# A hybrid recurrent layer on one core: the side chains between the projection matmuls are placed anew

## The chip, the core and the metric

One core of a Trainium2 chip runs the kernel. The metric is the device time of one execution in microseconds (us), the median of several runs; lower is better.

## What is computed

One step of a one-layer decoder on 2048 prompt tokens, 16 learned meta tokens in front of them, and 8 sample sequences of 4 tokens, at width 1024. The input is normalised, goes through one projection to the columns of four branches of width 256, each branch runs its own recurrence, is gated, and an output projection with a second normalisation ends the layer. All states go out too.

```python
hp = _layernorm(jnp.concatenate([meta, x_prompt], axis=1), ln_in_g, ln_in_b)
u = jnp.einsum('btd,de->bte', x, lw['w_in'])
...
# A: SSD, B: S5 diagonal SSM, C: gated DeltaNet, D: HGRN2; mix = their gated outputs
...
out = jnp.einsum('btc,cd->btd', mix, lw['w_out'])
x_new = _layernorm(DN_ALPHA * x + out, lw['ln_g'], lw['ln_b'])
```

Branch C, in a chunk, decays the products of its normalised keys and queries and inverts a triangular matrix:

```python
dec = jnp.exp(jnp.where(incl[:, :, None], diff, -jnp.inf))
kk = jnp.einsum('bcihd,bcjhd->bcijh', k, k)
m = jnp.where(strict[:, :, None], kk * dec * beta[:, :, :, None, :], 0.0)
tinv = lax.linalg.triangular_solve(eye + m, ...)
aq = jnp.einsum('bcihd,bcjhd->bcijh', q, k) * dec
```

Branch D multiplies queries and keys under a decay for each channel, and carries the state from chunk to chunk:

```python
a = jnp.einsum('bihk,bjhk,bijhk->bijh', qi, ki, dec)
o = (jnp.einsum('bijh,bjhv->bihv', a, vi)
     + jnp.einsum('bihk,bhkv->bihv', qi * jnp.exp(gi), s))
s = s * jnp.exp(gl)[..., None] + jnp.einsum('bjhk,bjhv->bhkv', ki * jnp.exp(gl[:, None] - gi), vi)
```

## The kernel before, in words

The tokens are worked off in two halves. Chunk 0 (48 tokens: meta tokens and all samples) and chunks 1 to 8 are the first half, chunks 9 to 16 the second. For each half `phase1a` normalises and transposes the input; `phase1b` runs the projection tile by tile (`proj`, L583): 128 output channels by blocks of some 300 to 512 tokens, 24 matmuls to a block (`pj`), each weight split into a high and a low part (L579, L580). Behind a block stand its consumers: the convolution and its activation (`conv_tile`, L641), copies to memory, gates. After both halves `out_chunk` runs the output projection.

Between the projection matmuls stand dependent chains of small work. They are generators, called jobs. A job yields the time until its next step may come, in microseconds of a planner's clock which adds an estimated cost for each TensorE instruction (`_pe`, L113); `poll` starts each step whose time has come, between two groups of three projection matmuls. So the yields set the place of each step among the matmuls. TensorE's instructions are pinned in the order in which they are written. The other engines and the DMA queue of SyncE are ordered by a scheduler, and each works off its own queue in order. When the program needs a job to be done, `drain` moves the clock on and puts the job's steps one behind the other, with no projection between.

The jobs that matter here:

- `gates` (L482): the gates of A and C for a half; sums of the logarithms over a chunk by TensorE (`g_g`), their exponentials as rows (`g_rw`), which go to memory as `rows_d`.
- `l2n` (L662): the norms of keys or queries of two heads: sums of squares (`l2p`), a power (`l2r`, L695 and L697), a transposition, a row to memory and back, a product (L713).
- `c_pre` (L730): for a pair of heads and each chunk, the decay matrix (`cdec`) is loaded from `rows_d`, masked on GpSimd (L725), exponentiated on ScalarE, and multiplied with the products of keys and queries (`cma`, L753); the result is stored to `ma_d`. After the second pair, `base_inv` (L761) loads the diagonal blocks of the matrices, inverts them on VectorE with two instructions per row (L787, L789), copies the result (L791) and stores it to `tb_d`. In the first half it does so twice, for the chunks ("main") and then for chunk 0 ("head").
- `right_jobs` (L1896): one sequence, each part behind the former: `b_setup` (branch B's matrices; the input matrices `W1` in four blocks `bs_wt`, L1070 to L1077), `b_tail` (chunk 0 of B), `b_main` (L1121 to L1169) twice, chunk 0 of D, D's groups of two chunks 1, 3, 5, 7, `b_main` twice, and in the second half D's groups 9 and 13 beside 11 and 15.
- `d_group` (L1576): D for a group. It loads queries with forget gates (`d_qf`), keys (`d_k`) and values, forms `d_pr` on GpSimd, the diagonal (`hsel`), and then goes through levels that double the block size: a product of `Q` and `d_k` on TensorE, a masked copy to `d_AT` (L1670), updates of `Q` and of the keys (L1666, L1667). Then for each chunk the keys are transposed and copied (`d_kt`), and outputs and the state `SD` follow. For chunk 0 `tail_state` (L1553) updates the nine segments' states in six parts: VectorE masks the values into a stage that takes `d_qf`'s buffer (L1564), one matmul (`d_qf`, `d_kt`), and an addition (L1573).

The last projection tile group of a half begins with a hook, `last`: it drains the inverse, in the first half also D's chunk 0, in the second half all of `right_jobs`.

Of the kernel before, what the change touches and what calls it, by code (L numbers as in the profile page):

```python
# [22 lines left out]
F32 = mybir.dt.float32  # L23
# [35 lines left out]
def tw(t):  # L59
    return 128 if t else HEAD  # L60
# [10 lines left out]
class Pinned:  # L71
    """An engine whose instructions don't move ahead of earlier ones."""
# [8 lines left out]
class Chain:  # L81
    """An engine whose instructions issued through here stay in the order in which they are written."""
# [14 lines left out]
class Kern:  # L97
# [12 lines left out]
    # The tensor engine runs in the order in which the kernel is written out. Dependent chains  # L110
    # are generators ("jobs") that yield the time until their next step can start; they are
    # woven between the matrix products of the projections.
# [64 lines left out]
    # ---------------------------------------------------------------- constants  # L177
    def consts(self, cp):
# [15 lines left out]
        # sums the two parts of 32 channels of a head  # L194
# [24 lines left out]
    # ---------------------------------------------------------------- phase 1  # L219
    def small_loads(self, cp):  # L220
        """Job: small parameters, and the conv histories of the sample sequences channel-major."""
        a, V = self.a, self.Vp
        yield 8.2
        # channel-major small parameters, through one transpose
# [29 lines left out]
        # HGRN2 lower bound: softmax over the single layer, cumulative sum minus the first entry  # L254
# [70 lines left out]
    def phase1a(self, half, xp):  # L325
        """Layer norm and transposition of the input, and the products whose results are wanted token-major.
        The first yield comes before anything that needs the space of xh, xl or the weight ring."""
# [46 lines left out]
        def weights(i, parts):  # L374
            """u | i, dt, a, b: high and low parts."""
# [23 lines left out]
        else:  # L399
            # the first tile waits for as little as possible: one row comes by DMA, the other through the tensor engine  # L400
# [81 lines left out]
    def gates_in(self, half, sp):  # L482
# [3 lines left out]
        o = 1 - half          # chunk 0, the tail, is the first of half 0  # L486
# [14 lines left out]
        # softplus = max(x, 0) + log1p(e), log1p(e) = 2 atanh(e / (2 + e))  # L501
# [20 lines left out]
        # beta = sigmoid  # L522
# [7 lines left out]
        # inclusive cumulative sums inside each chunk, and the chunk totals  # L530
        yield 19.0
# [19 lines left out]
        if o:  # L551
            # decays of the tail segments, on every partition
# [177 lines left out]
    def c_pre(self, p):  # L730
# [8 lines left out]
        for t in range(*TR[half]):  # L739
# [14 lines left out]
            for j in range(2):  # L754
                self.st(self.ma_d[t][:n, j, 2 * p:2 * p + 2, :n], ma[:n, j, :, :n])
# [1394 lines left out]
```

## Time and profile before

| | us |
|---|---|
| runs | 1456.67, 1447.78, 1452.73 |
| median | 1452.73 |
| span of the profiled execution | 1448.2 |
| TensorE busy | 1294.9 (89%) |
| VectorE busy | 934.2 (65%) |
| GpSimd busy | 616.3 (43%) |
| ScalarE busy | 536.1 (37%) |
| mean granted clock of TensorE | 0.936 of full speed |

The page does not list a time of the profiled execution besides its span; the span lies inside the range of the three runs. Busy time is the time in which an engine had an instruction at work. PE is TensorE, DVE VectorE, ACT ScalarE, POOL GpSimd, SP the engine that issues most transfers.

### The profile page before, as it was taken

Reading aid. Unit: us, or ns where it says so; the run is one execution under the profiler, and the core shown is the slowest. Engines: PE = TensorE matmul, PEld = TensorE weight load, DVE = VectorE, ACT = ScalarE, POOL = GpSimd, SP = SyncE. Lnnn points to the kernel's source line nnn. Section 1 sums busy time; section 2 is a strip of 40 time slices with the busy share of each in tenths; the row PEclk is TensorE's granted clock in tenths of the full one; section 3 lists DMA queues with packets and bytes.
Section 4 is the critical chain, followed back from the end, with each engine's and each line's share of the span. In section 5 each row is a group of like instructions: output and inputs, shape, how many; then the busy total and the mean of one; then the engine's idle time right before and its main releaser. Section 6 shows DMA issues by size and latency. Waiting matters only on the chain. (4 is left out here: it accounts for less than half of the span.)

```text
span 1448.2 us, 23800 instructions
## 1 busy us (share of the span) xinstructions
PE 1294.9 (89%) x8596; PEld 1090.3 (75%) x8596; DVE 934.2 (65%) x2173; ACT 536.1 (37%) x1010; POOL 616.3 (43%) x508
## 2 busy tenths in 40 slices
PE   7984898899898999998996888789997999999997
PEld 6974788878877999877674677677775677777776
DVE  8899524557978549474355789962345676665654
ACT  3224256545214342353543442242434332333211
POOL 4065322524433312152434443441324476676665
PEclk9997999999989999999998899899998899999999
DMA  8511552464337434215534633125649777676333
GB/s 211 192 49 36 127 143 57 140 189 114 106 97 203 145 104 153 77 39 158 157 87 121 201 102 95 44 88 145 177 124 251 196 198 190 198 182 184 111 105 113
DMA packets 259007, 195.79 MB, mean 135 GB/s; under 512 B 70950, under 2 KB 231928, under 8 KB 258873
## 3 DMA queue, kind: packets, MB, share of 16 engines
q1 hardware_dynamic: 258890, 194.28, 47.2%
q8 instruction: 68, 1.11, 0.3%
q14 instruction: 49, 0.39, 0.1%
HBM read 125.01 MB, written 64.31 MB: 131 GB/s over the span
## 5 line engine op out<-in xcount | busy, mean ns | idle before, releaser
L126 PE MATMUL pj<-xh,w 128*128 128x384 f32 (+2 forms) x1760 | 547.8, 379 | 10.8 <-ACT raw L635 5.5
L126 PEld LDWEIGHTS pj<-xh,w 128*128 128x128 f32 x1760 | 339.7, 200 | 57.4 <-issue 11.6
L126 PE MATMUL pj<-xl,w 128*128 128x384 f32 (+2 forms) x880 | 322.8, 367 | 0.0
L126 PEld LDWEIGHTS pj<-xl,w 128*128 128x128 f32 x880 | 176.3, 200 | 12.4 <-issue 0.5
L580 POOL TENSOR_TENSOR w<-wr,w 128x1024 fp32r<-128x1024 f32 x44 | 109.9, 2497 | 85.6 <-ACT w L579 68.0
L641 DVE SCALAR_TENSOR_TENSOR cv<-raw,par,cv 128x384 f32<-128x384 f32 (+2 forms) x150 | 130.5, 872 | 9.5 <-POOL cv L639 8.2
L126 PE MATMUL pj<-woh,o_mh 128*128 128x512 f32 (+2 forms) x280 | 116.6, 416 | 6.3 <-DVE xt L1846 3.2
L126 PE MATMUL pj<-wol,o_mh 128*128 128x512 f32 (+2 forms) x280 | 109.4, 391 | 6.2 <-POOL wol L1817 5.9
L126 PE MATMUL pj<-woh,o_ml 128*128 128x512 f32 (+2 forms) x280 | 109.4, 391 | 0.0
L126 PE MATMUL pj<-w,xh 128*128 128x256 f32 (+3 forms) x544 | 105.2, 295 | 0.0
L639 POOL TENSOR_SCALAR cv<-raw,par 128x384 f32<-128x384 f32 (+2 forms) x50 | 49.3, 986 | 119.0 <-ACT raw L635 95.4
L126 PEld LDWEIGHTS pj<-w,xh 128*128 128x128 f32 (+1 forms) x544 | 84.6, 189 | 1.2 <-ACT xh L88 0.8
L126 PE MATMUL pj<-w,xl 128*128 128x256 f32 (+3 forms) x272 | 78.0, 291 | 0.8 <-DVE xl L88 0.8
L725 POOL TENSOR_TENSOR cdec<-cdec,negm 128x256 f32<-128x256 f32 x32 | 29.4, 921 | 98.6 <-DMA cdec<-rows_d 63.1
L126 PEld LDWEIGHTS pj<-woh,o_mh 128*128 128x128 f32 (+1 forms) x280 | 52.3, 187 | 18.6 <-DVE xt L1846 4.0
L126 PEld LDWEIGHTS pj<-wol,o_mh 128*128 128x128 f32 (+1 forms) x280 | 52.5, 188 | 16.0 <-POOL wol L1817 6.9
L1789 DVE TENSOR_TENSOR y<-y,f_R 128x768 f32<-128x768 f32 (+1 forms) x17 | 27.1, 1591 | 56.0 <-POOL f_R L1788 50.9
L126 PEld LDWEIGHTS pj<-woh,o_ml 128*128 128x128 f32 (+1 forms) x280 | 52.2, 187 | 12.3 <-issue 0.7
L308 POOL TENSOR_TENSOR lnrs<-lnve,mhalf 128x1 f32<-128x1 f32 (+1 forms) x34 | 24.5, 720 | 74.0 <-DVE lnve L88 46.2
L813 ACT ACTIVATE zs<-pj 128x384 f32<-128x384 f32 (+2 forms) x40 | 20.8, 520 | 87.6 <-PE pj L126 72.8
L126 PEld LDWEIGHTS pj<-w,xl 128*128 128x128 f32 (+1 forms) x272 | 51.2, 190 | 1.5 <-DVE xl L88 1.3
L1788 POOL TENSOR_TENSOR f_R<-f_R,f_z 128x768 f32<-128x768 f32 (+1 forms) x17 | 30.2, 1778 | 51.1 <-DMA f_R<-r_d 32.5
(570 smaller groups left out, 2687.8 us busy)
## 6 DMA issues: line engine op xcount, KB each, us to landing
wr<-in_w_in_dram SPq DMA_DIRECT2D x46, 512.0 KB
xt<-in_x_prompt_dram SPq DMA_DIRECT2D x16, 512.0 KB
xn_d<-xt SPq DMA_DIRECT2D x16, 512.0 KB
ma<-cma SPq DMA_DIRECT2D x64, 128.0 KB
xt<-xn_d SPq DMA_DIRECT2D x16, 512.0 KB
out_dram<-xt SPq DMA_DIRECT2D x15, 512.0 KB
f_R<-r_d SPq DMA_DIRECT2D x32, 192.0 KB
cdec<-rows_d SPq DMA_DIRECT2D x32, 128.0 KB
```

The lines of the kernel that those rows point to most:

```text
L126: self._pe(self.PE.matmul(out, lhsT, rhs, start=start, stop=stop, **kw), 0.01 + n * (1 if rhs.dtype == F32R else 4) / 2400)
L308: self.G.tensor_tensor(rs[:n], ve[:n], self.mhalf[:n, 0:1], ALU.pow)
L580: self.G.tensor_tensor(w[:, :, 1], raw, w[:, :, 0].bitcast(F32), SUB)
L639: G.tensor_scalar(cv[:, 0:m], raw[:, 3:3 + m], w[3], b, op0=MUL, op1=ADD)
L641: V.scalar_tensor_tensor(cv[:, 0:m], raw[:, k:k + m], w[k], cv[:, 0:m], op0=MUL, op1=ADD)
L725: G.tensor_tensor(d[:n, :, :n], d[:n, :, :n], m[:n, None, :n].to_broadcast([n, nh, n]), ADD)
L813: S.activation(z, p, AF.Silu)
L1788: G.tensor_tensor(R[:, :, :n], R[:, :, :n], z[:, :, :n], MUL)
L1789: V.tensor_tensor(y6[:, 0:6, :n], y6[:, 0:6, :n], R[:, :, :n], MUL)
```

## The change

The decay of a chunk in `c_pre` is split in two: `decay_load` (the transfer) and `decay_end` (mask and exponential). The first chunk's is loaded and ended before the loop, and each further chunk's is loaded before the products of the former and ended behind them. In `d_group` the keys of all chunks of a group are transposed into one PSUM tile before the outputs; the first chunk's go into the buffer of `tots`. A group that follows another one waits 1.5 on the planner's clock before its first product, and not 8.0. Six yields of side chains are longer: the gates of the first half (19.0 to 25.0), `l2n` (3.7 to 6.0), the W1 blocks (2.6 to 6.5), `b_main` (17.1 to 19.5), D's step behind its first level (3.0 to 4.5), and `out_setup` for the first half of the output weights (8.9 to 16.0). Comments are taken out.

```diff
@@ gates
-        yield 19.0
+        yield 25.0 if o else 19.0
@@ l2n
-        yield 3.7
+        yield 6.0
         pt = self.pt()
         self.tr(pt[:2 * N, 0:128], rf)
@@ c_pre
-        yield 6.1
-        for t in range(*TR[half]):
+        a, b = TR[half]
+        raw = self.decay_load(self.fp, "cdec", a, 4 + 2 * p, 2)
+        yield 3.0
+        dec = self.decay_end(raw, a, 4 + 2 * p, 2)
+        yield 3.1
+        for t in range(a, b):
             n = tw(t)
             t0 = tof(t) - BASE[half]
-            dec = self.decay(self.fp, "cdec", t, 4 + 2 * p, 2)
-            yield 1.5
+            raw = self.decay_load(self.fp, "cdec", t + 1, 4 + 2 * p, 2) if t + 1 < b else None
...
+            if raw is not None:
+                yield 1.0
+                dec = self.decay_end(raw, t + 1, 4 + 2 * p, 2)
+                yield 1.5
@@ b_setup, the W1 blocks
             V.tensor_tensor(wt, wt, wu, ADD)
-            yield 2.6
+            yield 6.5
@@ b_main
-        yield 17.1
+        yield 19.5
@@ d_group
-        yield 13.6 if tail else 8.0
+        yield 13.6 if tail else 8.0 if first else 1.5
...
-            yield 3.0
+            yield 4.5 if s == 2 else 3.0
...
-        else:
+        kts = [tots[:, :, 0:128]] * (nch - 1) + [tp.tile([128, 2, 128], F32, name="d_kt" + sfx)]
+        p = self.pt()
+        for c in range(nch):
+            for g in range(2):
+                self.tr(p[:n, 256 * c + 128 * g:256 * c + 128 * g + 128], kS[:, g, n * c:n * c + n])
+            S.copy(kts[c][:n], p[:n, 256 * c:256 * c + 256].rearrange("p (g d) -> p g d", g=2))
+        yield 1.4
+        if not tail:
             yield from self.until(("d", t0c))
         for c in range(nch):
             t = t0c + c
             tk = slice(n * c, n * c + n)
-            p = self.pt()
-            for g in range(2):
-                self.tr(p[:n, 128 * g:128 * g + 128], kS[:, g, tk])
-            kt = tp.tile([128, 4, 64], F32, name="d_kt" + sfx)
-            S.copy(kt[:n].rearrange("p h d -> p (h d)"), p[:n, 0:256])
-            yield 1.4
+            kt = kts[c]
@@ out_setup
-            yield 8.9
+            yield 16.0 - 7.1 * half
@@ right_jobs
         def seq(ts, sfx):
-            for t in ts:
-                yield from self.d_group(t, 2, sfx)
+            for i, t in enumerate(ts):
+                yield from self.d_group(t, 2, sfx, i == 0)
```

On TensorE, early in the first half, the gates' sums (`g_g`), their rows (`g_rw`) and the W1 transposes (`bs_wt`) stand before as follows; `w_1229` and `w_1491` are the weights of two projection tiles that follow each other.

```order
L126 MATMUL pj<-xh,w_1229 128x384
L126 MATMUL pq<-g_g_1270,triu 128x64
L126 MATMUL pq<-g_g_1270,ones 128x64
...
L120 MATMUL pq<-ident,bs_wt 128x128 x4
...
L120 MATMUL pq<-ident,g_rw 128x128
L126 MATMUL pj<-xh,w_1229 128x384
...
L120 MATMUL pq<-ident,bs_wt 128x128 x4
```

Now, in the same stretch:

```order
L126 MATMUL pj<-xh,w_1491 128x304
L120 MATMUL pq<-ident,bs_wt 128x128 x4
L126 MATMUL pq<-g_g_1270,triu 128x64
L126 MATMUL pq<-g_g_1270,ones 128x64
...
L126 MATMUL pq<-l2p,sel_140 32x9 x8
...
L120 MATMUL pq<-ident,g_rw 128x128
...
L120 MATMUL pq<-ident,g_rw 16x128
L120 MATMUL pq<-ident,bs_wt 128x128 x4
```

All of them move behind matmuls of the next tile, the gates' sums 33 projection matmuls later, the four W1 blocks 27, 48, 69 and 93 later.

Late in the first half, on TensorE, D's chunk 0 (the transposes of its keys, its outputs with the state `S`, and the six products `d_qfa,d_kta` of `tail_state`) stands before like this; the five products that are left out here follow with 8 to 12 projection matmuls in front of each.

```order
L120 MATMUL pq<-ident,d_ka 48x128 x2
L126 MATMUL pj<-xh,w_4032 128x384
...
L126 MATMUL pq<-d_ATa,d_va 64x48 x4
L126 MATMUL pq<-d_pra,S_3929 128x16
...
L126 MATMUL pq<-d_qfa,d_kta 128x384
L126 MATMUL pj<-xh,w_4032 128x384
L126 MATMUL pj<-xl,w_4032 128x384
...
L126 MATMUL pq<-d_qfa,d_kta 128x384
```

Now:

```order
L126 MATMUL pq<-Qa,d_ka 16x16 x2
L120 MATMUL pq<-ident,d_ka 48x128 x2
L126 MATMUL pq<-d_ATa,d_va 64x48 x4
L126 MATMUL pq<-d_pra,S_4138 128x16
L126 MATMUL pq<-d_pra,S_4138 128x4 x8
L126 MATMUL pq<-d_pra,S_4138 128x16
L126 MATMUL pq<-d_pra,S_4138 128x4 x8
L126 MATMUL pq<-d_qfa,d_kta 128x384 x6
L126 MATMUL pj<-xh,w_4320 128x304
```

The last level, the transposes, the outputs and all six products stand together, at the place of the hook `last`, and no projection matmul is between them.

On VectorE at the same place, the end of the main inverse (128 partitions), the masks of `tail_state` (`d_qfa<-d_va,segmask`) and the head inverse (12 partitions) now come in this order:

```order
L803 TENSOR_TENSOR acc<-acc,cdec 128x31
...
L1587 TENSOR_TENSOR S_4138<-S_4138,pq 64x3x64 x2
L1578 TENSOR_TENSOR d_qfa<-d_va,segmask 48x384
L801 TENSOR_TENSOR cdec<-acc 12x15
L803 TENSOR_TENSOR acc<-acc,cdec 12x15
...
L801 TENSOR_TENSOR cdec<-acc 12x48
L1587 TENSOR_TENSOR S_4138<-S_4138,pq 64x3x64
L803 TENSOR_TENSOR acc<-acc,cdec 12x12x4
L1587 TENSOR_TENSOR S_4138<-S_4138,pq 64x3x64
L1578 TENSOR_TENSOR d_qfa<-d_va,segmask 48x384
```

Before, all six masks stood in front of the first operation of the head inverse; now four of them stand behind it.

## Rows read from the trace of the kernel before

**Rows 1.** Page, busy us, share of the span, instructions of an engine.

```profile
PE 1294.9 (89%) x8596; PEld 1090.3 (75%) x8596; DVE 934.2 (65%) x2173; ACT 536.1 (37%) x1010; POOL 616.3 (43%) x508
```

**Rows 2.** Waits of TensorE by what it waited for: us in total, times, longest.

```profile
PE pq L126 <- DVE Qa L1666: 16.7, 10, 6.4
PE pq L120 <- DVE bs_wt L1072: 13.3, 3, 8.3
PE pq L126 <- DVE b L1152: 12.2, 2, 9.2
PE pq L120 <- DVE l2r L697: 8.5, 3, 4.6
PE pq L126 <- DVE g_g L521: 7.4, 1, 7.4
...
PE pq L126 <- DVE cma L753: 5.7, 4, 2.4
...
PE pq L120 <- POOL l2r L695: 3.1, 1, 3.1
...
PE pq L126 <- DVE SD L1712: 3.0, 1, 3.0
```

**Rows 3.** Windows: length, busy us of each engine (instructions), granted clock, DMA share, GB/s.

```profile
100.00:125.00 25.00, 14.04 (x65) 12.51 (x63) 23.29 (x81) 9.59 (x20) 15.80 (x28) 0.80 0.08 21
125.00:150.00 25.00, 12.78 (x79) 11.58 (x79) 24.98 (x68) 11.34 (x22) 14.30 (x6) 0.80 0.14 37
...
350.00:375.00 25.00, 24.67 (x142) 22.04 (x140) 24.69 (x63) 9.83 (x21) 13.79 (x10) 1.00 0.48 143
375.00:400.00 25.00, 21.59 (x129) 20.23 (x129) 24.37 (x67) 6.89 (x21) 8.48 (x9) 0.83 0.24 76
...
1325.00:1440.00 115.00, 111.84 (x661) 90.56 (x659) 65.94 (x130) 23.92 (x30) 71.23 (x45) 1.00 0.39 118
```

**Rows 4.** Timeline of TensorE after the gates' sums: start, us, instruction.

```profile
120.84 0.84 PE L126 MATMUL pj<-xh,w 128*128 128x384 f32 x2
121.48 0.52 PE L126 MATMUL pj<-xl,w 128*128 128x384 f32 x1
...
122.39 0.52 PE L126 MATMUL pj<-xh,w 128*128 128x384 f32 x2
122.75 0.34 PE L126 MATMUL pj<-xl,w 128*128 128x384 f32 x1
```

**Rows 5.** Timeline of VectorE between 124 and 141 us.

```profile
124.00 5.43 DVE L641 SCALAR_TENSOR_TENSOR cv<-raw,par,cv 128x328 f32<-128x328 f32 x1
129.35 2.82 DVE L1072 TENSOR_TENSOR bs_wt<-bs_wt,bs_wu 128x512 f32<-128x512 f32 x1
...
140.65 0.67 DVE L1072 TENSOR_TENSOR bs_wt<-bs_wt,bs_wu 128x512 f32<-128x512 f32 x1
```

**Rows 6.** Timeline of GpSimd in the same stretch.

```profile
124.03 5.05 POOL L1061 TENSOR_TENSOR Pw<-Pw,bs_w 128x2304 f32<-128x2304 f32 x1
129.03 2.60 POOL L580 TENSOR_TENSOR w<-wr,w 128x1024 fp32r<-128x1024 f32 x1
```

**Rows 7.** Timeline of TensorE at D's chunk 0; in brackets the idle time before.

```profile
377.79 0.43 PE L126 MATMUL pq<-Qa,d_ka 128*48 128x48 f32 x4 [3.12 <-DVE Qa L1666]
...
413.25 0.88 PE L126 MATMUL pq<-d_qfa,d_kta 48*128 48x384 f32 x2 [1.95 <-DVE d_qfa L1564]
...
416.03 0.91 PE L126 MATMUL pq<-d_qfa,d_kta 48*128 48x384 f32 x2
...
418.64 0.91 PE L126 MATMUL pq<-d_qfa,d_kta 48*128 48x384 f32 x2
```

**Rows 8.** Timeline of VectorE: the main inverse's last operation, the head inverse's first.

```profile
407.50 0.19 DVE L789 TENSOR_TENSOR acc<-acc,cdec 128x31 f32<-128x31 f32 x1
...
419.19 0.16 DVE L787 TENSOR_TENSOR cdec<-acc 12x15 f32<-12x15 f32 x1
```

More of the change, by code (lines that the diff above doesn't have):

```diff
@@ L718, in decay, with decay_load @@
     def decay(self, pool, tag, t, rows0, nh, bufs=None):
-        S, G = self.S, self.G
+        return self.decay_end(self.decay_load(pool, tag, t, rows0, nh, bufs), t, rows0, nh)
+    def decay_load(self, pool, tag, t, rows0, nh, bufs=None):
         n = tw(t)
@@ L723, in decay, with decay_end @@
         self.ld(d[:n, :, :n], dap(self.rows_d, (t * 16 + rows0) * 128, [[0, n], [128, nh], [1, n]]))
+        return d
+    def decay_end(self, d, t, rows0, nh):
+        S, G = self.S, self.G
+        n = tw(t)
         m = self.negm if t else self.negm_t
@@ L1574, in tail_state, with d_group @@
                 yield 1.4
-    def d_group(self, t0c, nch, sfx):
+    def d_group(self, t0c, nch, sfx, first=True):
         V, S, G = self.V, self.S, self.G
@@ L1707, in d_group @@
                 for g in range(2):
-                    self.mm(su[:, g], kt[:n, 2 * g:2 * g + 2].rearrange("p h d -> p (h d)"), vf[:n, 128 * g:128 * g + 128])
+                    self.mm(su[:, g], kt[:n, g], vf[:n, 128 * g:128 * g + 128])
                 for g in range(2):
@@ L1731, in d_group @@
                 V.tensor_copy(cdd[:, :, 1:9], tot4[:, :, 4:12])
-                yield from self.tail_state(self.SD9, kt, vf,
+                yield from self.tail_state(self.SD9, kt.rearrange("p g (h d) -> p (g h) d", h=2), vf,
                                 lambda h, g: cdd[64 * h:64 * h + 64, g, :, None],
```

## Prediction, before the changed kernel ran

> **What bounds the kernel now.** I read the busy shares first, then the tensor engine's waits, then windows of 25 us, then single engines inside the windows that stand out. The shares say that TensorE is the bound: 89% of the span, against 65% for VectorE [rows 1]. Its instructions run in the order in which they are written, so a microsecond of its idleness is gained back only if the matmuls behind it move up. In the last stage it is busy 111.84 of 115 us at a granted clock of 1.00 [rows 3]; what is saved before comes out at the end. The waits name what the change aims at: Qa (the levels of branch D), bs_wt (the input matrices W1 of branch B), b (B's states), l2r (the norms), g_g (the gates), cma (the products of branch C) and SD (D's state) [rows 2]. The windows add a warning. Between 100 and 150 us TensorE is busy only 26.8 of 50, but VectorE 48.3, and between 350 and 400 VectorE is busy 49.1 of 50 [rows 3]. In such stretches TensorE waits because VectorE is late, and moving the waiting instruction back helps only as far as other matmuls don't depend on the same VectorE.
>
> **The change part by part.** All terms are in us on the profiled execution, whose page gives the span of 1448.2 alone; the three timed runs have a median of 1452.73, 4.5 above it.
>
> *Gates and W1, early.* Gone or moved: 7.4 (g_g) and 13.3 (bs_wt, three times), 20.7 together [rows 2]. The order shows the gates' sums behind 33 projection matmuls more, the W1 transposes behind 27 to 93 more. A pair of them lasts 0.84 us where one alone lasts 0.52, so they start 0.32 apart; two microseconds later it is 0.52 and 0.34, so 0.18 apart [rows 4]: half clock and full clock. At 0.18 the delays are 6 us for the gates and 5 to 17 for W1. But VectorE has the same 48 us to do. In its new order the copy that feeds g_rw stands some thirty rows of other work behind g_g, so I put a new wait of about 11 us on the g_rw transposes in its place. Net -10. Bounds: nothing gained, if VectorE sets this whole stretch, and 28 if all 20.7 go with the half-clock work after them. That work is visible in the same rows: six us after the wait on g_g the matmuls still start 0.32 us apart, which is some 3 us lost.
>
> Row first, for a rule on this place: the addition that ends a W1 block took 2.82 us at 129.35 and 0.67 at 140.65, and a convolution step 5.43 [rows 5]; the slow ones lie beside GpSimd's sum Pw (5.05) and its weight split (2.60) [rows 6]. The Trainium skill, SBUF — State Buffer, section "Who interferes with whom", says that a VectorE instruction with two SBUF inputs contends with a GpSimd instruction that reads SBUF, and that the second waits for the first to end. The trace agrees. By that rule a W1 addition may fall under Pw instead of under the weight split and this term would be about -8 instead of -10.
>
> *Norms.* l2r waits 8.5 in three places on VectorE and 3.1 once on GpSimd [rows 2]. The step is put 2.3 us later on the planner's clock, and in the second half the order leaves 27 matmuls instead of 9 or 15 between. Taking at most 2.3 to 3 from each: -8 (bounds 0 and -11.6).
>
> *States of B.* b waits 12.2 in two places, the longest 9.2 [rows 2]. Put 2.4 later: the short one (3.0) goes, the long one loses 2 to 3. -5 (bounds 0, -12).
>
> *Levels of D.* Qa waits 16.7 in ten places, the longest 6.4; one is the 3.12 at 377.79 [rows 2, 7]. The longer step after the first level lets twelve more matmuls in before the second, 2 us for each of three groups that wait there: -6 (bounds 0, -16.7).
>
> *Decay rows of C a chunk ahead.* The transfer, GpSimd's mask and the exponential leave the loop between two chunks. cma waits 5.7 in four places [rows 2], and part of it is the multiplication itself, which stays: -3 (bounds 0, -5.7).
>
> *Keys together, groups at once.* The same transposes and copies run, in one stretch rather than two; I put this itself at nothing, since neighbours cover them (bounds +2 and -2). D's chain ends earlier, so that the half's end need not drain it: SD's 3.0 [rows 2] go, -3. In return the next group's first product stands 21 to 30 matmuls behind the last of the former, and GpSimd must form d_pr in that time; where a weight split of 2.60 [rows 6] is in front, it is late. For three groups +2 (bounds 0, +8).
>
> *D's tail.* This is the price. B now delays D, and the diff's own delays add to it: the first product of chunk 0 moves five blocks of 24 matmuls back. Before, the six state updates stand with 8 to 12 matmuls between them. Now the last level, the transposes, the outputs and all six updates stand together in the drain that ends the first part, with no projection between. One update takes 2.61 from start to start (416.03 to 418.64), of which TensorE works 0.91 [rows 7], while VectorE adds the result and masks the next part: five gaps of 1.7 are 8.5 us idle. VectorE's order makes it worse: four of the six masks stand behind the first operation of the inverse for chunk 0, which waits until the main inverse has been copied, stored and read back. That took 11.5 us before (407.50 to 419.19) [rows 8]. About 6 us of other work stand in that gap now, so some 5 are added, and 3 for the last level and the transposes without cover: 16.5. What goes in return is 3.12 and 1.95 of idle time [rows 7] and less half-clock work, together 6.5. Net +10 (bounds 0 and +30, the latter if the main inverse is still running when TensorE arrives).
>
> *Output weights.* One step later on the planner's clock; the transfers that limit them are not moved. 0 (bounds -3, +3).
>
> Sum: -10 - 8 - 5 - 6 - 3 - 3 + 2 + 10 = -23, so 1425 for the span and, 4.5 above it, 1430 for the median.
>
> On the clock: the granted clock is 0.80 in the two windows with the long waits and 1.00 in the last stage [rows 3], that is, a part of them at 1.2 GHz and the rest at 2.4. The Trainium skill, TensorE: Matmul & The Clock Gate, section "HAM oscillation — how this bites in real kernels", says that an engine which waits falls back to the lower clock and pays for it in the work behind. By that rule a vanished wait gives more than its length, and the sum would be near -30; but the new drain would be charged the same way, and the trace shows both.
>
> **The rivals.**
> 1. *All named waits vanish.* Gates, W1, norms, b's short wait, D's levels and SD give 20.7 + 11.6 + 5 + 10 + 3, and TensorE, whose work is 1294.9 [rows 1], simply closes up; the drain costs 10. That is -40, a median of 1412. For it: VectorE has 35% of the span free. Against it: not where these waits are [rows 3].
> 2. *VectorE keeps its pace.* The matmuls are written earlier or later, but between 100 and 150 and between 350 and 400 VectorE finishes when it did. Early gains (-10, -8 in half) are then waited out at the next consumer, and what is left, some -12 of the later terms, pays the drain: 1450. For it: 48.3 and 49.1 busy of 50 [rows 3]; against it, VectorE has room over the whole span [rows 1], so that a stretch which ends late is made up behind it.
> 3. *The drain swallows it: slower.* TensorE comes to the drain earlier by the 15 to 20 us gained, while the main inverse, which VectorE works off in one piece with little spare, ends when it did, at 407.5 [rows 8]. TensorE then waits these 15 to 20 out as well, adds 16.5 of drain and some 5 of half-clock work, and only the later terms (about -12) stand against it: +15 to +20 once the upstream gain is gone, a median near 1468. It decides from where TensorE arrives more than some 15 us before the inverse's last operation. Against it: the inverse also waits for fewer competitors, since D's tail no longer lies inside it.
> That the change does not do what it says I leave out: the order shows each part.
>
> **How the numbers follow.** The forecast (-10 to -32) gets 0.50, rival 1 0.12, rival 2 0.24, rival 3 0.14. About 1% (14.5 us) is what a measurement of this kernel can tell from no change. Faster by more: four fifths of the forecast's case, all of rival 1 and a little of rival 2, 0.54. Slower by more: most of rival 3, 0.12. Within: 0.34. The likeliest case's own range is 1420 to 1444; the wide one runs from 1405 (rival 1 with some of the clock) to 1462 (the lower half of rival 3).
>
> **What would show it.** Right: g_g and bs_wt gone from the list of waits with one on g_rw of 5 to 15 in their place; l2r under 4; the wait on b under 8; Qa under 10; and a new group of waits on d_qfa and S inside one stretch of some 25 us, late in the first half, where projections stop. Wrong: no such stretch, or one of 40 us with the wait on the inverse's operations; a span of 100 to 150 that is as long as before (rival 2); waits on d_pr of more than 8 in all.

## The result, and the profile after

The changed kernel is slower: 1515.54 us (1514.12 to 1518.32), against 1454.7 for the kernel before (1447.78 to 1461.62), a ratio of 1.043 with an interval of 1.037 to 1.050. Its profiled execution has a span of 1513.9, 65.7 more than the 1448.2 of before. The forecast was 1430 with a range up to 1462.

The page's first part, to be read beside [rows 1]:

```profile
span 1513.9 us, 23785 instructions
...
PE 1316.2 (87%) x8596; PEld 1104.7 (73%) x8596; DVE 936.7 (62%) x2173; ACT 558.8 (37%) x1027; POOL 621.8 (41%) x508
```

TensorE has the same 8596 matmuls and is busy 21.3 us longer with them, at a mean granted clock of 0.913 instead of 0.936; the other 44 us of the 65.7 are idle. ScalarE is busy 22.7 longer, with 17 instructions more.

The waits of TensorE (us in total, times, longest), against [rows 2]:

```profile
PE pq L126 <- DVE l2p L683: 22.5, 2, 20.5
PE pq L126 <- DVE Qa L1680: 21.8, 10, 7.2
PE pq L126 <- DVE acc L713: 13.2, 4, 7.2
PE pj L126 <- ACT raw L635: 13.0, 4, 4.2
PE pq L120 <- DVE b L1135: 12.7, 3, 7.6
PE pq L120 <- DVE l2r L697: 9.0, 1, 9.0
PE pq L120 <- ACT d_tota L1701: 7.8, 6, 3.1
```

Three of them in the kernel before, beside [rows 2]:

```profile
PE pj L126 <- ACT raw L635: 5.5, 2, 3.1
...
PE pq L120 <- DVE b L1121: 4.2, 1, 4.2
...
PE pq L126 <- DVE acc L713: 1.4, 1, 1.4
```

The list is the main reading. Five of the names that the change aimed at are gone or nearly so: g_g (7.4 before), bs_wt (13.3), cma (5.7) and the b that was 12.2 are no longer listed, and SD fell from 3.0 to 0.4. Qa and l2r stayed: Qa rose from 16.7 to 21.8, l2r has 9.0 where it had 8.5 and 3.1. And other waits came up or grew: l2p has 22.5, about the 20.7 of g_g and bs_wt together; b at an earlier step of its chain rose from 4.2 to 12.7; acc, the product that ends the norms, from 1.4 to 13.2; raw, a copy on ScalarE, from 5.5 to 13.0; d_tota, another copy on ScalarE, is new with 7.8. That l2p stands in the place of g_g and bs_wt is shown below and in run 15; for the other pairs it is likely and not shown.

The early stretch, in windows (columns as in [rows 3]), and TensorE and VectorE inside it:

```profile
100.00:125.00 25.00, 18.45 (x105) 17.20 (x104) 25.00 (x79) 8.78 (x18) 19.23 (x31) 0.93 0.08 21
125.00:150.00 25.00, 5.90 (x34) 5.79 (x35) 22.40 (x66) 11.44 (x20) 9.35 (x3) 0.53 0.11 31
```

```profile
119.79 0.33 PE L126 MATMUL pq<-g_g,triu 128*128 128x64 f32 x2
...
144.10 0.43 PE L126 MATMUL pq<-l2p,sel 128*32 128x9 f32 x16 [20.50 <-DVE l2p L683]
...
146.54 0.41 PE L120 MATMUL pq<-ident,g_rw 128*128 128x128 f32 x1
```

```profile
124.25 5.59 DVE L970 TENSOR_TENSOR cosT<-cosT,bur 128x256 f32<-128x256 f32 x2
...
143.49 0.55 DVE L683 TENSOR_REDUCE l2p<-sq 128x12 f32<-128x384 f32 x1
```

TensorE runs through the gates' sums without a stop and is idle for most of the second window instead. VectorE is busy 47.4 of the 50 us, nearly as before (48.3), and starts the reduction that the norms need (l2p) only at 143.49.

At the drain late in the first half, TensorE and then VectorE:

```profile
431.37 0.25 PE L126 MATMUL pq<-Qa,d_ka 128*16 128x16 f32 x4 [1.64 <-DVE Qa L1680]
...
444.18 1.61 PE L126 MATMUL pq<-d_qfa,d_kta 48*128 48x384 f32 x2 [1.65 <-DVE cdec L801]
...
456.78 1.62 PE L126 MATMUL pq<-d_qfa,d_kta 48*128 48x384 f32 x2 [1.56 <-DVE d_qfa L1578]
458.33 0.62 PE L126 MATMUL pj<-xh,w 128*128 128x304 f32 x1
```

```profile
436.12 0.18 DVE L803 TENSOR_TENSOR acc<-acc,cdec 128x31 f32<-128x31 f32 x1
...
443.96 0.15 DVE L801 TENSOR_TENSOR cdec<-acc 12x15 f32<-12x15 f32 x1
...
446.69 0.55 DVE L1578 TENSOR_TENSOR d_qfa<-d_va,segmask 48x384 f32<-48x384 f32 x1
```

From 431.37 to 458.33 no projection runs: 27 us. An update takes 3.15 from start to start (444.18 to 456.78 are four), and its matmul 1.62, where [rows 7] have 0.91. The granted clock is 0.50 here, the lower of TensorE's two levels; before, it was 1.00 from 416.03 to 418.64, between the last two updates:

```profile
444.18:458.33 14.15, 8.01 (x11) 2.46 (x11) 10.36 (x42) 0.00 (x0) 0.81 (x1) 0.50 0.13 28
```

To see where time is lost, I count TensorE's projection matmuls in its timeline and take the start of every 24th (a block). The table gives the start of some blocks minus that of the same block in the kernel before, in us of the profiled executions: block 25 lies behind the gates, 58 in front of D's chunk 0, 67 behind the drain, 108 behind D's groups, 132 at the end of the second half, 162 behind the first chunks of the output stage, 178 at the end. All rows but the first are of the experiments below. Two cautions. Each row is one execution, and those of one kernel differ: the kernel before took 1445.86 to 1463.83 us, and its profiled execution is among the shorter ones, so the last column is 1 to 17 us above the differences of medians. Runs 6, 9, 10, 12 and 13 have all matmuls in the order of before up to block 58 and are yet 2.9 to 5.9 behind there; so much needs no cause in TensorE's order. And the count leaves out the side matmuls, all those that aren't projections. In front of blocks 67, 132, 162 and 178 every run has as many of them as before (to within one). In front of 25 and 26 the runs that delay the gates and W1 have up to 46 fewer, in front of 58 the changed kernel, yields_only and no_out have 48 fewer, and in front of 108 the runs lie between 56 fewer (drain_only, early_only, early_l2p) and 80 more (d_only). At those blocks a part of the difference is work that has been moved, not time gained or lost.

| run | 25 | 26 | 58 | 67 | 108 | 132 | 162 | 178 |
|---|---|---|---|---|---|---|---|---|
| changed kernel | -20.2 | -0.9 | 14.2 | 33.8 | 37.6 | 37.0 | 63.8 | 65.4 |
| parts_only | 0.6 | 0.3 | 18.8 | 17.4 | 29.3 | 22.0 | 28.2 | 29.4 |
| yields_only | -18.0 | -1.8 | 28.6 | 42.3 | 43.9 | 56.7 | 78.5 | 80.9 |
| no_w1 | -5.3 | -5.1 | 21.6 | 22.4 | 31.5 | 33.9 | 58.9 | 61.8 |
| no_out | -20.1 | -2.0 | 15.4 | 36.8 | 42.2 | 43.9 | 56.7 | 58.5 |
| c_only | 0.8 | 0.8 | 23.5 | 22.1 | 29.1 | 33.9 | 36.2 | 38.5 |
| d_only | 1.0 | 0.3 | 5.0 | 4.8 | 29.2 | 30.8 | 50.9 | 51.7 |
| early_only | -21.5 | -1.3 | 42.7 | 54.7 | 40.0 | 57.6 | 62.0 | 63.8 |
| control | 0.3 | -0.5 | 14.4 | 10.9 | 13.5 | 24.1 | 35.9 | 38.7 |
| control_mirror | 1.7 | 1.0 | 10.1 | 9.2 | 13.7 | 13.7 | 21.1 | 23.5 |
| drain_only | 1.0 | 0.3 | 2.9 | 19.7 | 9.1 | 22.8 | 34.2 | 36.4 |
| groups_apart | 1.2 | 0.5 | 5.9 | 5.8 | 9.7 | 15.9 | 24.5 | 26.6 |
| only_out | 0.1 | 0.4 | 3.6 | 3.1 | 0.2 | 5.4 | 24.9 | 24.3 |
| keys_copies_after | 1.5 | 1.8 | 6.0 | 3.5 | 6.4 | 7.8 | 20.3 | 22.2 |
| c_whole | 1.0 | 0.4 | 17.7 | 20.3 | 30.7 | 34.1 | 37.5 | 38.6 |
| early_l2p | -20.3 | -13.0 | 32.0 | 45.5 | 34.7 | 48.5 | 52.9 | 54.9 |

Read along the first row: the changed kernel is 20 us ahead at block 25 and level one block later. By block 67, with the drain and the side matmuls that were moved into it, it is 34 behind, by 132 another 3, and it loses 27 in the output stage, where the forecast had put a zero.

### The profile page after: what moved, and what is told of

Same layout as the page of the kernel before. It is cut to its first block, busy times and chain, and to the rows that moved or that the text cites. A ratio compares the mean times of both kernels' runs of the same rounds, so it can differ in the third digit from the quotient of the medians.

```text
span 1513.9 us, 23785 instructions
## 1 busy us (share of the span) xinstructions
PE 1316.2 (87%) x8596; PEld 1104.7 (73%) x8596; DVE 936.7 (62%) x2173; ACT 558.8 (37%) x1027; POOL 621.8 (41%) x508
## 4 chain that ended last, share of the span: by engine, by line
PE 41%; DVE 22%; DMA 14%; issue 7%; POOL 6%; ACT 6%; SPq 3%; POOLq 0%; DVEq 0%; ACTq 0%
PE pj L126 25%; PE pq L126 14%; DVE cv L641 5%; PE pq L120 3%; DMA cdec<-rows_d 2%; DMA f_R<-r_d 2%; DVE Qa L1680 1%; DMA b<-b 1%; DMA a_L<-rows_d 1%; POOL f_R L1805 1%; DVE cdec L801 1%; DVE acc L803 1%; DVE y L1806 1%; DVE xt L88 1%; POOL cv L639 1%
## 5 line engine op out<-in xcount | busy, mean ns | idle before, releaser
L126 PEld LDWEIGHTS pj<-xh,w 128*128 128x128 f32 x1760 | 343.4, 202 | 65.1 <-ACT raw L635 14.3
L126 PE MATMUL pj<-xl,w 128*128 128x384 f32 (+2 forms) x880 | 326.1, 371 | 0.0
L126 PEld LDWEIGHTS pj<-xl,w 128*128 128x128 f32 x880 | 178.5, 203 | 13.2 <-issue 0.5
L580 POOL TENSOR_TENSOR w<-wr,w 128x1024 fp32r<-128x1024 f32 x44 | 114.3, 2598 | 89.0 <-ACT w L579 72.9
L641 DVE SCALAR_TENSOR_TENSOR cv<-raw,par,cv 128x384 f32<-128x384 f32 (+2 forms) x150 | 131.7, 880 | 19.6 <-POOL cv L639 18.1
L639 POOL TENSOR_SCALAR cv<-raw,par 128x384 f32<-128x384 f32 (+2 forms) x50 | 48.5, 970 | 129.8 <-ACT raw L635 77.3
L126 PEld LDWEIGHTS pj<-woh,o_mh 128*128 128x128 f32 (+1 forms) x280 | 53.2, 190 | 21.3 <-ACT woh L1833 8.0
L126 PE MATMUL pq<-Qa,d_ka 128*128 128x128 f32 (+2 forms) x256 | 36.7, 287 | 21.8 <-DVE Qa L1680 21.8
```

Source lines behind the costliest of these rows:

```text
L126: self._pe(self.PE.matmul(out, lhsT, rhs, start=start, stop=stop, **kw), 0.01 + n * (1 if rhs.dtype == F32R else 4) / 2400)
L580: self.G.tensor_tensor(w[:, :, 1], raw, w[:, :, 0].bitcast(F32), SUB)
L639: G.tensor_scalar(cv[:, 0:m], raw[:, 3:3 + m], w[3], b, op0=MUL, op1=ADD)
L641: V.scalar_tensor_tensor(cv[:, 0:m], raw[:, k:k + m], w[k], cv[:, 0:m], op0=MUL, op1=ADD)
```

## The experiments

Theory 1 was that the six longer yields do the harm, by pushing D's chunk 0 into the drain; theory 2 that the three structural parts do it.

**1. The structural parts alone (parts_only).** The changed kernel with six yields set back:

```diff
-        yield 25.0 if o else 19.0
+        yield 19.0
...
-            yield 16.0 - 7.1 * half
+            yield 8.9
```

> The changed kernel with its six longer yields set back: the decay rows of C a chunk ahead, D's keys together and D's groups at once are left. Theory 1 (the loss of some 61 us comes from the later steps, above all from branch B, which pushes D's chunk 0 into the drain): the tail of D stands among projections again, 1440 to 1458, the time of before or a little less. Theory 2 (the loss comes from D's groups following at once and from the longer loop of C, whose two yields of 1.0 and 1.5 replace one of 1.5): 1485 to 1510.

1483.74, ratio 1.020 (1.014 to 1.027). Between the two forecasts: the parts alone cost 2%, and D's tail stands among projections.

**2. The yields alone (yields_only)**, on the kernel before.

> The kernel before with the six longer yields alone. Theory 1: 1495 to 1520, nearly the whole loss, with the stretch without projections in the drain of some 30 us. Theory 2: within 15 us of 1453.

1527.82, ratio 1.050 (1.046 to 1.054): more than the whole change. The yields do most of the harm, but 2.0% and 5.0% don't add up to 4.3%: the parts don't act one by one.

**3. The W1 blocks set back (no_w1)**, on the changed kernel.

```diff
-            yield 6.5
+            yield 2.6
```

> The changed kernel with the yield of the W1 blocks alone set back to 2.6. The order then leaves the six state updates of D's chunk 0 among the projections (blocks 63.75 to 65.75). Theory 1: most of the loss of the first half goes, 30 to 40 us, a time of 1475 to 1487; what is left sits in the second half and in the output stage. Theory 2: less than 10 us are gained, 1505 or more.

1505.24, ratio 1.035 (1.030 to 1.039). The drain's step is gone, as the table shows (21.6 at block 58, 22.4 at 67), but only 10 us of the time. Theory 1 falls as the whole story: at block 67, where both runs have done the same work, 22.4 of the changed kernel's 33.8 are left with D's tail out of the drain. (The 14.2 at block 58 can't be set beside the 21.6: the changed kernel has 48 side matmuls fewer in front of it.)

**4. The output weights set back (no_out)**, on the changed kernel.

```diff
-            yield 16.0 - 7.1 * half
+            yield 8.9
```

> The changed kernel with the yield of the output weights alone set back to 8.9. If this yield costs what the stage from the last projections to block 162 lost between the two profiles (46 to 64 us behind, 18), the time is 1497 or so, and the order of the C steps at the start of the output stage is that of before; if that stage is slow for another reason (the state in which the transfers and GpSimd reach it), nothing changes, 1510 to 1520.

1510.43, ratio 1.039 (1.034 to 1.043); the intervals of this and of the changed kernel overlap, so the verdict on the time is open. The stage itself lost 13 between blocks 132 and 162 and not 27.

That left a third theory, here called theory 0: the order of the kernel before is one that suits the engines unusually well, and any displacement costs. The next runs put it against single causes.

**5. C's decay rows alone (c_only)**, on the kernel before (the part of `c_pre` in the diff above).

> The kernel before with C's decay rows a chunk ahead alone. Theory C (the two decay buffers now hold one chunk in use and one in transfer, so that GpSimd's mask and ScalarE's exponential, each in its queue, stand in front of other work and wait for the transfer; the products of projections behind them are copied out late): about the 20 us that the three parts together lost by block 48, a time of 1470 to 1480. Theory 0 (any displacement of the order costs this much): 1465 to 1485, and the control the same. Neither: 1450 to 1460.

1488.34, ratio 1.020 (1.015 to 1.025). ScalarE and TensorE around 205 us show how it goes wrong:

```profile
203.69 0.70 ACT L734 ACTIVATE cdec<-cdec,nac 128x128 f32<-128x128 f32 x2 [7.74 <-POOL cdec L732]
...
211.75 0.69 ACT L734 ACTIVATE cdec<-cdec,nac 128x128 f32<-128x128 f32 x2 [4.26 <-POOL cdec L732]
212.46 1.28 ACT L834 ACT_TABLE_LOAD   x1
213.75 0.49 ACT L834 ACTIVATE zs<-pj 128x384 f32<-128x384 f32 x1
```

```profile
214.30 0.44 PE L126 MATMUL pj<-xh,w 128*128 128x384 f32 x1 [3.60 <-ACT zs L834]
```

The copy `zs`, for which the projections wait 3.60, stands in ScalarE's queue behind an exponential that waits for its mask, and behind a table load of 1.28. But all waits on `zs` at this line are 6.5 us, where the run is 25 behind at block 48. Whether this or mere displacement makes the rest was then still open (run 14).

**6. D's keys and groups alone (d_only)**, on the kernel before.

> The kernel before with D's keys together and its groups at once alone; nothing differs before block 67 or so. If the three parts are additive and C's costs some 20, this one costs 5 to 10 in all: it loses some 15 between blocks 70 and 92, where the groups stand closer, and gains some 15 at the end of the second half, where D's chain is no longer drained: 1450 to 1465.

1496.89, ratio 1.025 (1.018 to 1.032): a miss by 32 us. No matmul moves before block 67, as said; then 26 are lost between blocks 67 and 132, and 20 in the output stage, whose code and order on TensorE are the same.

**7. The two early yields alone (early_only)**, on the kernel before.

> The kernel before with the two early yields (gates 25.0, W1 blocks 6.5) alone; the order puts D's chunk 0 into the drain (block 66.00). Theory 1: 25 to 45 us slower than before, 1480 to 1500, with some 20 us of it between blocks 58 and 67, and the early gain of some 20 at block 25 given back by block 26. Theory 0: 15 to 30 slower wherever the steps stand, without a step at 66.

1512.3, ratio 1.037 (1.032 to 1.042), beyond the expected time. Ahead by 21.5 at block 25, level at 26, 42.7 behind at 58, where the expectation had nearly nothing, and only 12 more at 67. Some 32 of the 42.7 come between blocks 48 and 58. This stretch holds 88 side matmuls that stood earlier before, and 22 us more idle time; the largest piece of that is one wait:

```profile
395.70 0.69 PE L126 MATMUL pq<-Pw,b 128*64 128x128 f32 x4 [14.84 <-DVE b L1152]
```

```profile
394.09 0.40 DVE L787 TENSOR_TENSOR cdec<-acc 128x231 f32<-128x231 f32 x1
394.41 1.24 DVE L1152 TENSOR_TENSOR b<-b,b 128x1040 f32<-128x1040 f32 x1
395.56 0.39 DVE L789 TENSOR_TENSOR acc<-acc,cdec 128x231 f32<-128x231 f32 x1
```

B's states, which come later by the W1 yields, have slipped into the main inverse on VectorE (L787 and L789, here from 371.46 on). Before, this step stood at 334.95, the inverse began at 349.98, and TensorE waited 2.97.

**8. A control (control)**, three yields of the kernel before moved by little:

```diff
-        yield 19.0
+        yield 18.6
...
-        yield 3.7
+        yield 3.9
...
-        yield 17.1
+        yield 16.8
```

> The kernel before with three yields moved by little and both ways (gates 19.0 to 18.6, norms 3.7 to 3.9, branch B 17.1 to 16.8): the order changes slightly in many places and nothing is gained or lost by intention. Theory 0 (the order of before was chosen among many by measuring, so that any displacement costs 1 to 2%): 1465 to 1485. Otherwise 1448 to 1460.

1482.13, ratio 1.017 (1.012 to 1.022). A change with no aim costs 22 us (the kernel before, timed beside it, took 1460.38). Its page:

```profile
PE 1308.8 (88%) x8596; PEld 1099.9 (74%) x8596; DVE 929.7 (63%) x2173; ACT 539.7 (36%) x1011; POOL 619.6 (42%) x508
```

With the same work TensorE is busy 13.9 longer than in [rows 1] (clock 0.923 for 0.936) and idle for the rest of the difference. The yields moved by little, but the order did not: 1366 of the 4300 side matmuls have another number of projection matmuls in front of them, up to 36 fewer.

**9. The drain alone (drain_only).** D's chunk 0 later, on the kernel before, nothing else:

```diff
-        yield 13.6 if tail else 8.0
+        yield 32.0 if tail else 8.0
```

> The kernel before with one yield changed: the first product of D's chunk 0 waits 32.0 instead of 13.6, so that its tail falls into the drain (block 66.00) and nothing in front of block 58 moves. If the drain is what costs the changed kernel most: equal to before up to block 58, 15 to 30 us behind at block 67, 1475 to 1490 in all. If the drain is cheap, because TensorE's projections close up in front of it, and the displacement alone costs: less than 8 us at block 67.

1484.94, ratio 1.020 (1.013 to 1.027). This is the clean one: 2.9 behind at block 58, 19.7 at 67. TensorE there:

```profile
412.15 0.27 PE L126 MATMUL pq<-Qa,d_ka 128*16 128x16 f32 x4
...
428.93 1.62 PE L126 MATMUL pq<-d_qfa,d_kta 48*128 48x384 f32 x2 [5.61 <-DVE cdec L787]
...
441.32 1.61 PE L126 MATMUL pq<-d_qfa,d_kta 48*128 48x384 f32 x2 [1.49 <-DVE d_qfa L1564]
```

The wait of 5.61 ends with the head inverse's operation (cdec), as the forecast had it for the mask behind it. Between the starts of blocks 58 and 67 TensorE has the same 296 matmuls before (first row) and here (second):

```profile
367.41:429.22 61.81, 56.12 (x296) 48.70 (x295) 54.14 (x137) 13.15 (x37) 24.06 (x24) 0.86 0.37 105
```

```profile
370.31:448.92 78.61, 58.74 (x296) 49.40 (x295) 63.65 (x164) 13.77 (x39) 27.67 (x25) 0.78 0.36 104
```

So the drain costs 16.8 us: 14.2 more idle time (19.9 for 5.7) and 2.6 more busy time, at a lower clock. The loss stays. At block 108 the run is only 9.1 behind, but 56 side matmuls are still to be done there; at 132, with the same work done, it is 22.8 behind.

**10. Keys together, groups apart (groups_apart)**, on the kernel before.

> The kernel before with D's keys together and the groups 8.0 apart as before. If the start of a group right behind the former is what costs in the run with both (24 us between blocks 67 and 92): less than 8 us in that stretch, 1460 to 1475. If the keys in one stretch cost it (one PSUM tile with four transposes, the copies on ScalarE): 15 to 25 in that stretch, 1480 to 1500.

1473.03, ratio 1.011 (1.005 to 1.017), inside the first range; the stretch between blocks 67 and 92 lost 10.8, with 16 side matmuls more in it, between the two forecasts. If the two parts add, 1.4% of run 6's 2.5% are left for the groups at once: given the intervals, the halves can't be told apart. A small wait is new:

```profile
PE pq L120 <- ACT d_tota L1687: 5.0, 6, 1.6
...
PE pq L120 <- ACT d_totb L1687: 1.0, 2, 0.5
```

**11. The control mirrored (control_mirror)** (19.4, 3.5, 17.4).

> The first control's three small displacements with the opposite sign (19.4, 3.5, 17.4). If the order of before is one picked out among many, so that any displacement costs: 1470 to 1490, slower like the first control. If the first control was slower because of the sign of its changes: equal to before or faster, 1440 to 1458.

1472.84, ratio 1.011 (1.008 to 1.014). Slower with either sign: both controls fall where theory 0 put them, and the sign is not the cause. This one is small in its order too: 405 side matmuls move, nearly all of them by three projection matmuls. TensorE's busy time is again 11.2 above [rows 1]:

```profile
PE 1306.1 (89%) x8596; PEld 1100.1 (75%) x8596; DVE 934.4 (64%) x2173; ACT 541.3 (37%) x1014; POOL 615.2 (42%) x508
```

**12. The output weights alone (only_out)**, on the kernel before (the diff's edit of `out_setup`).

> The kernel before with the longer yield of the output weights alone; nothing changes in front of the output stage, where C's first step and all that hangs on it move by some projection matmuls. If this yield is what makes the output stage 18 us longer in the changed kernel: equal to before up to block 132, 12 to 20 behind at block 162, 1467 to 1478. As forecast before (nothing, since the weights' transfers set that stage): 1451 to 1460.

1473.4, ratio 1.011 (1.006 to 1.017). 5.4 behind at block 132, 24.9 at 162. The waits of the stage:

```profile
1143.39 0.66 PE L126 MATMUL pj<-woh,o_mh 128*48 128x512 f32 x1 [4.52 <-ACT woh L1816]
...
1150.79 0.66 PE L126 MATMUL pj<-woh,o_mh 128*48 128x512 f32 x1 [3.77 <-ACT woh L1816]
...
1250.43 1.06 PE L126 MATMUL pq<-c_T,c_MT 32*32 32x32 f32 x30 [4.30 <-DVE c_vn L1468]
...
1290.29 1.06 PE L126 MATMUL pq<-c_T,c_MT 32*32 32x32 f32 x30 [3.85 <-DVE f_r L1767]
```

Only the first two are waits for weights. The others sit 100 us further on, in C's chain: one step moved at the start shifts the places of all that follow. The weights' transfers (`xt`) are shifted too. On SyncE, before:

```profile
1125.53 0.90 SPq L1814 DMA_DIRECT2D xt<-in_w_out_dram  x2
...
1131.85 0.53 SPq L1814 DMA_DIRECT2D xt<-in_w_out_dram  x1
```

In this run:

```profile
1131.07 2.46 SPq L1384 DMA_DIRECT2D c_N<-tb_d  x5
1133.95 0.39 SPq L1814 DMA_DIRECT2D xt<-in_w_out_dram  x1
...
1143.55 0.38 SPq L1814 DMA_DIRECT2D xt<-in_w_out_dram  x1
```

The sixth transfer of weights is issued 8.4 later than before, behind five of C's, and the last 11.7 later, though the run is only 5.4 behind at block 132. In all, TensorE waits hardly longer for the weights (10.2 for 9.3). Of the 19.5 us that the stage lost, 12.7 are idle time and the rest busy time.

**13. Keys together, copies behind all transposes (keys_copies_after)**, on run 10's kernel:

```diff
         for c in range(nch):
             for g in range(2):
                 self.tr(p[:n, 256 * c + 128 * g:256 * c + 128 * g + 128], kS[:, g, n * c:n * c + n])
+        for c in range(nch):
             S.copy(kts[c][:n], p[:n, 256 * c:256 * c + 256].rearrange("p (g d) -> p g d", g=2))
```

> D's keys together and groups 8.0 apart, but with all four transposes of a group in front of the two copies. In the run with transposes and copies in turn, the second pair of transposes waits in eight places for ScalarE's copy of the first (6.0 us in all), which stands in the same PSUM tile. If that wait is what the gathered keys cost: the waits on d_tot vanish, 4 to 8 us faster than that run's 1473, 1465 to 1470. If the displacement costs, not the wait: the waits vanish and the time stays, 1470 to 1480.

1470.34, ratio 1.009 (1.006 to 1.012), run 10 had 1.011 (1.005 to 1.017). The waits on d_tot are gone from the list and the time can't be told from run 10's. The wait was real, and it is not what the gathered keys cost.

**14. C's decay whole, one chunk ahead (c_whole)**, on the kernel before:

```diff
-            dec = self.decay(self.fp, "cdec", t, 4 + 2 * p, 2)
-            yield 1.5
+            nxt = self.decay(self.fp, "cdec", t + 1, 4 + 2 * p, 2) if t + 1 < b else None
...
+            dec = nxt
+            if dec is not None:
+                yield 1.5
```

> The kernel before with C's whole decay (transfer, mask, exponential) one chunk ahead, in one piece and with one yield of 1.5 per chunk as before; the place of the products among the projections is then nearly that of before. If the split cost the 25 us (mask and exponential placed behind the products, and 2.5 instead of 1.5 per chunk, so that the second buffer's transfer, the mask and the exponential follow each other within each chunk and copies of projections stand behind an exponential that waits): at most 10 us behind at block 48, 1455 to 1470. If any such displacement costs as much: 18 to 28 behind at block 48, 1475 to 1490.

1491.34, ratio 1.024 (1.020 to 1.028), 20 behind at block 48 (start of that block against before's, as in the table; 32 side matmuls more stand in front of it) and 18 at 58. The split is not the cause; having the decay a chunk ahead costs in either form. Whether the two buffers are at fault, which a third would tell, wasn't tried.

**15. The early yields with the norm's sums later (early_l2p)**, on run 7's kernel:

```diff
-        yield 6.1
+        yield 30.0 if (half, key) == (0, 'k0') else 6.1
```

> The run with the two early yields, and the first norm's sums (l2p) another 24 on the planner's clock later, so that they stand at block 28.00 and not at 25.12, behind the place where TensorE waited 20.5 us for them. If VectorE sets the stretch from 100 to 150 us, the wait only moves to the next instruction that needs it (the rows g_rw, or a W1 block), and block 30 comes within 6 us of before. If the wait was the fault of this one place: block 30 comes 12 to 20 us earlier than before. The end is not the question: D's tail falls into the drain as there, 1500 to 1520.

1505.23, ratio 1.033 (1.029 to 1.036). The wait of 20.5 has split and moved:

```profile
135.27 0.45 PE L120 MATMUL pq<-ident,g_rw 128*128 128x128 f32 x1 [10.20 <-DVE g_rw L563]
157.81 0.43 PE L126 MATMUL pq<-l2p,sel 128*32 128x9 f32 x16 [9.60 <-DVE l2p L683]
```

Together 19.8, and block 30 starts 4.1 us ahead of before. This is within the margin that the expectation named: VectorE sets that stretch.

## Why the prediction was wrong

The forecast was 23 us less; the change costs 61 more by the medians. Four steps of its sum failed: the early "Net -10", of which 0.9 was left at block 26; waits booked as time gained; the 6.5 that the drain was to give back, which did not come; and the zero for the output weights, where 27 were lost.

*The reading of the bound was right, the use of it was not.* The forecast says that in a stretch where VectorE is nearly always busy, moving TensorE's waiting instruction back does not help, and then books -10 there. The trace: 20 us ahead at block 25, 0.9 at 26. The new wait came on l2p with 20.5 and not on g_rw with 11; run 15 shows that with l2p out of the way g_rw takes 10.20, very near to the forecast's number for it, and l2p another 9.60. The step that failed here is "Net -10": it gave back 11 of the 20.7 at one consumer, where VectorE, with 48 us of work in 50, takes back all at two.

*The terms of a few microseconds were added as if they were independent.* Each was the length of a wait that would go, and two waits did go, on cma and SD. The levels' wait grew instead (Qa 21.8 for 16.7, with -6 booked); the norms' fell by 2.6 (-8 booked) while acc, in the same job, took 11.8 more; of the waits on b the one of 12.2 went and an earlier one grew to 12.7. And a wait that goes is not time gained: C's decay alone costs 2.0% where -3 us was booked, with bounds of 0 and -5.7; D's keys and groups cost 2.5% where +2 and -3 were. The edits don't add either: at block 67 the run with C's decay alone is 22.1 behind, the one with the two early yields alone (and the drain that follows from them) 54.7, and the changed kernel, which has both, 33.8. The sum has no term for what a displaced order costs as such. The two controls put a size to it: 1.1% and 1.7%, 17 and 22 us by the medians, for three yields moved by 0.2 to 0.4 us. Rival 2 (VectorE keeps its pace) came nearest for the early part; no rival had this cost.

*The drain came where it was forecast, at more than its price.* D's tail stood in the drain, without projections for 27 us (the forecast said some 25). Net +10 was booked, from 16.5 of idle time less 6.5 that was to come back. Run 9 measures 16.8. The idle time in its drain (blocks 64 to 67) is 16.6, just as booked; the term that failed is the return. Outside the drain only 2.4 of idle time went (5.7 to 3.3), since another wait, 3.3 on raw, took the place of the old ones. And TensorE had no less half-clock work but more: 2.6 us of busy time were added. Part of the 16.5 is luck. Its largest piece, five gaps of 1.7, was taken from 416.03 to 418.64 of [rows 7], where TensorE has no gap: it runs projections between the two updates and is busy for the whole 2.61.

```profile
416.03:418.64 2.61, 2.61 (x13) 1.82 (x12) 2.50 (x8) 0.18 (x1) 1.38 (x3) 1.00 0.44 132
```

That VectorE's addition and mask then left gaps of 1.5 to 1.65 in the drain agrees by luck: the forecast had shown no such gap. The 19.6 of the changed kernel between blocks 58 and 67 hold 48 side matmuls more and can't be read as the drain's price. The window from 421 to 460 there has a granted clock of 0.62:

```profile
421.00:460.00 39.00, 26.53 (x100) 18.81 (x101) 33.24 (x102) 5.10 (x14) 11.68 (x12) 0.62 0.35 102
```

The 5 us for the head inverse in front of four masks did not show in the changed kernel, where 7.8 us (436.12 to 443.96) were filled by other work; in run 9 it is within the 5.61, some 4 above the gaps of 1.5 that follow. Rival 3 named the drain as the place of a loss, but by another way: TensorE, 15 to 20 us early, was to wait for the main inverse. TensorE came to block 65 at 423.3, 1.6 us later than before; the inverse did end later, at 436.30 (before at 407.69, [rows 8]), but behind it TensorE was busy with the outputs until 440.88 and did not wait for it.

*"Output weights: 0."* This is the largest single miss: the changed kernel lost 26.7 between blocks 132 and 162. The argument was that the weights' transfers set the stage and are not moved. Run 12, whose order is that of before up to this stage, is 18 us slower by the medians and loses 19.5 here: by this edit alone the transfers move, and with them the steps of branch C and the whole weave of the stage. Not all of the 26.7 need be this edit's: with the yield set back (run 4) the stage still lost 12.8.

*What stays open.* Why displacements like the controls' cost 17 to 22 us is not traced to one mechanism; the slip of B's states into the inverse in run 7 is one that a trace shows. In the controls, 13.9 of 38.3 and 11.2 of 23.1 us between the profiles are more busy time at a lower clock, the rest idle time in many small waits. A lower clock of the whole run does not explain it: where the kernel before itself had a mean granted clock of 0.922 to 0.926 in an execution, it took 1459.32 to 1463.83 us, the first control at the same clocks 1481.52 to 1488.6 and the mirrored one 1472.1 and 1473.38. Nor is TensorE's order all. In the twelve runs without the edit of the output weights the matmuls of the output stage have exactly the order of before, and the stage is 2.3 to 20.0 us longer in every one. The other engines' order differs there in some places, and the profiled execution of before is a short one; how much each accounts for was not tested. That the kernel before sits at a good order is what nine runs with a part of the change or a few small edits say (5, 6, 8 to 14: all slower, by 0.9 to 2.5%); how it came there, no run can tell.

## What to carry to other kernels

Where in-order engines are woven together by hand-set delays, first run a control: move a few delays slightly, both ways. If that already costs 1 to 2%, waits of a few microseconds in the profile are not independent terms, and a sum over them can't be trusted to that much; what counts is the whole order, and it has to be measured. A wait whose releaser is an engine without spare time in that stretch need not go away when the waiting instruction is moved back: between 100 and 150 us here it came up at the next consumers with its full length. And an estimate of idle time must be taken from a place where the engine is idle: the distance of two instructions may be filled by others.

## What was not expected of the hardware

One long wait pulls its surroundings down: in the window from 125 to 150 us of the changed kernel the granted clock is 0.53. Behind the wait of 20.50, from 144.10 to 150.28, TensorE is busy without a gap and still at the lower level:

```profile
144.10:150.28 6.18, 6.18 (x35) 6.06 (x36) 3.42 (x9) 2.33 (x3) 3.24 (x1) 0.50 0.06 15
```

And gaps need not be long: in the drain, with gaps of 1.5 to 1.65 between matmuls of 1.62, the clock stays at 0.50 for 14 us (444.18 to 458.33). The same 8596 matmuls took between 1294.9 (before) and 1316.2 us (after), 1.6% apart, with their places changed and not their work; the mean granted clock of the changed kernel was 0.911 to 0.917 in its four runs, that of before 0.922 to 0.937 in the runs that list it. On VectorE two products took 5.59 us beside GpSimd's sum Pw, as a convolution step had in [rows 5, 6]. This is in line with the rule of the Trainium skill that the forecast drew on (SBUF — State Buffer, section "Who interferes with whom"). The two products stand in VectorE's queue in front of the copy for the gates' rows and of the reduction at 143.49 that the norms waited for.
